# Padding split weight tiles and every second split residual tile by 64 bytes

## The chip, the cores and the metric

The kernel runs on one core of one Trainium2 chip. The time is the device time of one execution in microseconds, from the first to the last instruction with what lies around them. The engines are TensorE (PE, with its weight loads shown apart as PEld), VectorE (DVE), ScalarE (ACT), GpSimd (POOL) and SyncE (SP, which issues DMAs). On-chip memory (SBUF) has 128 partitions; an address below is the byte offset within a partition.

## The reference

512 tokens of 1024 channels in float32 pass through three blocks: a block of two layers with recurrent mixers, a block with two kinds of attention, and a block with latent attention and a convolution branch. Almost all of the arithmetic is products of the normed tokens with weight matrices:

```python
def conv_glu(u, w_in, conv_w, conv_b, w_out):
    gate, val = jnp.split(u @ w_in, 2, axis=-1)
    return (jax.nn.silu(dwconv_centred(gate, conv_w, conv_b)) * val) @ w_out
...
    for i in range(DEPTH):                      # first block
        u = rmsnorm(h, norm1_w[i])
        ... h = h + hgrn2_mixer(u, ...)  or  h + mamba2_mixer(u, ...)
        h = h + conv_glu(rmsnorm(h, norm2_w[i]), ffn_w_in[i], ...)
...
        x = x + jnp.square(jax.nn.relu(h @ w_ff1[i])) @ w_ff2[i]    # second block
...
    a, b = jnp.split(h @ w_13, 2, axis=-1)      # third block, swiglu
    return (jax.nn.silu(a) * b) @ w_2
```

## The kernel before

Channels lie on partitions: the residual is eight tiles `x0` to `x7` of 128 channels by 512 tokens. A float32 product is made from two parts of each operand in the type float32r, high and low: `split` (L241) has ScalarE copy a tile into the high part (L242) and VectorE subtract it from the source into the low part (L243). For the residual these are `xh` and `xl`, eight tiles each, made by `split_tiles` (L272) in the pool `res`; within the feed-forward stages the hidden tiles are `hh` and `hl`, elsewhere `yh`/`yl`, `ogh`/`ogl`, `mh`/`ml`, `mg`, `at`, `oah`/`oal`, `obh`/`obl`, `qah`/`qal`, each in a pool of its stage.

Weights come by `chunk` (L161): one DMA of up to 512 KB into `raw` (128 partitions by 1024 elements, three buffers), then the split into `whi` and `wlo` (three buffers each, used in turn), all in the pool `wp`. `accumulate` (L181) then makes for each k-tile three matmuls into one PSUM bank: `whi` against `xh` (L188), `whi` against `xl` (L189), `wlo` against `xh` (L190). The weights are loaded into the array (128 by 128); the residual tile streams past, 512 columns. Every matmul has a weight load of its own. `tok_unit` (L1098) does it the other way round for a few products: the token tile is loaded and the weights stream, 256 columns (L1110 to L1112), and `products_n` has the same three lines as L1595 to L1597.

All of it is written out as a straight program; the order of PE's instructions is that of the calls, and buffers are waited for where they come round again.

Where tiles lie in SBUF follows from the sizes alone. Pools are laid out in the order in which they are opened, within a pool the tags in the order of their first use, and each tag's buffers side by side, rounded to 32 bytes. `const` comes first, then `res` (`x0` to `x7`, then `xh` 0, `xl` 0, `xh` 1, `xl` 1 and so on, 2048 bytes each), `wp` (`raw`, `whi`, `wlo`, 4096 bytes each), `tp` (temporaries), and then the pool or pools of the running stage. All of `res` and `wp` are multiples of 512 bytes, so `xh`, `xl`, `raw`, `whi` and `wlo` all start at the same place mod 512. The small tiles in `tp` add up to 192 over a multiple of 512, and some stages open small tiles ahead of their large ones. Counted from the place of `whi`, mod 512 bytes:

| tiles | place |
|---|---|
| `x`, `xh`, `xl`, `raw`, `whi`, `wlo` | 0 |
| `yh`, `yl` (mamba, 320 bytes of small tiles ahead) | 0 |
| `hh`, `hl` of `conv_glu` and `relu_ffn`; `mh`, `ml`, `mg`, `at`, `oa`, `ob`, `kvh`, `kvl` | 192 |
| `qah`, `qal` (64 bytes of small tiles ahead) | 256 |
| `hh`, `hl` of `swiglu` (128 bytes of small tiles ahead) | 320 |
| `ogh`, `ogl` (192 bytes of small tiles ahead) | 384 |

Of the kernel before, what the change touches and what calls it, by code (L numbers as in the profile page):

```python
# [9 lines left out]
F32R = mybir.dt.float32r  # L10
# [6 lines left out]
P = 128  # L17
D = 1024
NT = 512
# [3 lines left out]
WSZ = 1024  # L23

# Vectors over channels, kept as columns [128, rows] after a transpose on chip.
# [16 lines left out]
def view(t, off, dims):  # L42
    """The tile's partitions with another pattern of its free elements."""
    return bass.AP(t.tensor, t.offset + off, [t.ap[0], *dims])


def tree_masks():
    """masks[l][s, t]: s and t lie in different halves of one block of 2 ** (l + 1) tokens."""
    import numpy as np

    a = np.arange(P)
    out = np.zeros((8, P, P), np.float32)
    for l in range(7):
        half = a >> l
        out[l] = (half[:, None] ^ half[None, :]) == 1
    return out


def bucket_rows():
    """Rows of buckets against places: place w holds the bias of distance 255 - w; the last row  # L60
    masks the places outside the window."""
    import numpy as np

    out = np.zeros((33, 384), np.float32)
    for w in range(384):
        d = 255 - w
        if not 0 <= d < 128:
            out[32, w] = -1e30
            continue
        b = d if d < 16 else min(31, 16 + int(math.log(d / 16) / math.log(8) * 16))  # L70
        out[b, w] = 1.0
    return out


def rope_consts():
    """The signed swap of channel halves (transposed, for two heads of 64) and cos, sin by channel."""
# [17 lines left out]
class Net:  # L94
# [66 lines left out]
    def chunk(self, w, k0, nk, *segs):  # L161
        """Rows k0.. (nk tiles of 128) of w and the columns in segs (start, count), side by side,
        split into two float32r parts."""
# [5 lines left out]
        hi = self.wp.tile([P, WSZ], F32R, tag="whi", name=self.nm("whi"), bufs=3)  # L169
        lo = self.wp.tile([P, WSZ], F32R, tag="wlo", name=self.nm("wlo"), bufs=3)  # L170
# [10 lines left out]
    def accumulate(self, ps, tile, m, xs):  # L181
        """Add the products of one weight tile's 128 columns m to ps[feature, token]."""
# [9 lines left out]
    def products(self, tiles, m, xs, evac):  # L192
        """evac(psum[feature, token]) of the 128 columns m of weight tiles [(first k, count, parts)]."""
# [5 lines left out]
    def units(self, w, xs, n0, ncols, evac, k0=0):  # L199
        """The calls that make evac(psum, m) for each tile of 128 columns of w: psum[feature, token]  # L200
        over the k-tiles xs; one call for each load of weights."""
# [4 lines left out]
        for c0 in range(n0, n0 + ncols, wide):  # L206
            nn = min(wide, n0 + ncols - c0)

            def unit(c0=c0, nn=nn):
# [4 lines left out]
                # A load is done with before the next one's turn, for all of its columns.  # L214
# [17 lines left out]
    def load(self, w, nk, *segs):  # L232
        """Weight tiles for products: all nk k-tiles of the columns segs."""
# [12 lines left out]
    def begin_norm(self, wname=None, wj=0, via=None, pool=None):  # L246
        """Start of a norm's statistics; prep(j) then takes each tile of x as it is ready, and
        splits its product with the norm's weights where wname is given. via: the weights of a
        norm in between, whose result x becomes (through, once end_norm has its statistics)."""
# [22 lines left out]
    def split_tiles(self, j):  # L272
        h = self.res.tile([P, NT], F32R, tag=f"xh{j}", name=self.nm("xh"))
        l = self.res.tile([P, NT], F32R, tag=f"xl{j}", name=self.nm("xl"))
        return h, l

    def through(self):
        """x becomes the result of the norm in between."""
# [20 lines left out]
    def rsqrt(self, out, v, n):  # L299
        """out = v ** -0.5 on [128, n] columns, with a Newton step."""  # L300
# [9 lines left out]
    def bcast_cols(self, out, cols, nt=4):  # L310
        """[128 tokens, nt] columns to rows [128, nt * 128] that are the same on every partition."""
# [8 lines left out]
    def end_norm(self, want_bc=True, beside=None):  # L320
        """rsqrt(mean(x * x) + eps): columns [128 tokens, 4], and the same broadcast over partitions;
        with a norm in between, both norms' factors together. beside: other work, to go between."""
# [13 lines left out]
        if self.via:  # L336
            # 1 / sqrt(v) / sqrt(s / v + eps) = 1 / sqrt(s + eps * v)
# [14 lines left out]
    def load_x(self, x, *first):  # L352
        """x with channels on partitions. first: weights to load and split on the way."""
# [225 lines left out]
    def gla_steps(self, hp, masks, S, h):  # L579
        """Both directions of one head, in steps that other work may go between.  # L580
        f: [backward, forward] decays; kk: [forward, backward] keys.
        In a chunk of 128 tokens att[s, t] is the sum over channels of q[t] k[s] and the decays between
        the two, found by halves: a pair (s, t) belongs to the one block of 2m tokens in whose halves
        it lies apart."""
# [17 lines left out]
        while m < P:  # L602
            # Keys that the two halves' queries meet, side by side.
# [32 lines left out]
        # Between chunks of 128 tokens by the states that enter them.  # L636
# [35 lines left out]
        # The head's norm, with tokens on partitions; then its gate, and split for the product behind.  # L672
# [22 lines left out]
    def mamba(self, nxt):  # L695
# [6 lines left out]
        with ExitStack() as st:  # L702
# [4 lines left out]
            # silu(t) = h * (1 + tanh(h)) with h = t / 2: the norm's factor and the conv's bias carry the half.  # L707
# [12 lines left out]
            for d, sg in ((0, 1), (1, -1)):  # L720
                # Forward keeps keys s <= t, backward s >= t.
# [25 lines left out]
            def project(g):  # L747
                """The calls that make the group's B, C, x and gate, one for each 128 columns."""
# [44 lines left out]
            def scale(js):  # L793
                """The later groups' operands carry the norm's factor."""
# [22 lines left out]
            while ended < G:  # L817
# [11 lines left out]
                # The last group's chain keeps some for its end.  # L829
# [8 lines left out]
    def mamba_decays(self, mc, mp, dram, w_in, xw, rhalf):  # L838
        """Step sizes and decays of all heads: rows hold [half of the tokens, direction, head]."""
        nc, I = self.nc, self.I  # L840
        H2, NH = 64, NT // 2
        # The heads' columns twice: every half of the rows has all tokens, and keeps its own.
# [24 lines left out]
        # log(1 + e) = 2 atanh(s), s = e / (2 + e) <= 1 / 3, by its series.  # L867
# [16 lines left out]
        # Sums of the log decays in each chunk of 128 tokens, up to t (forward) and from t on (backward).  # L884
# [3 lines left out]
        for hs in halves:  # L888
# [5 lines left out]
            # A chunk's whole sum, for each direction.  # L894
# [18 lines left out]
        # The same with tokens on partitions: [token, chunk, (direction, head)].  # L913
# [8 lines left out]
        # exp of the chunks' sums on every partition.  # L922
# [14 lines left out]
    def ssd_steps(self, mp, g, r, dec, tri, dsk, yo):  # L937
        """Four heads that share B and C: both directions' scans by chunks, the gate and the norm,
        in steps that other work may go between."""
# [15 lines left out]
        def weights(w, hd):  # L955
            """exp(-relu(cum[s] - cum[t])) times the masked products of C and B."""
# [7 lines left out]
        # Tokens on partitions.  # L964
# [12 lines left out]
        # Products of C and B inside each chunk, for the two directions.  # L977
# [11 lines left out]
        def scaled(name, c, dirs, bufs):  # L989
            """x times a factor of each token and head, for the directions dirs."""  # L990
# [10 lines left out]
        # States that enter each chunk.  # L1001
# [96 lines left out]
    def tok_unit(self, w, segs, xs, scale, out):  # L1098
        """out[c][token, column]: the product with tokens on partitions, scaled by token, for the
        256 columns segs."""  # L1100
# [15 lines left out]
    def attention2(self, nxt):  # L1116
# [5 lines left out]
        with ExitStack() as st:  # L1122
# [8 lines left out]
            with ExitStack() as st2:  # L1131
# [22 lines left out]
                def do_wq(i):  # L1154
                    # Window heads i and i + 4 share a tile, so that each lies beside its keys.
# [75 lines left out]
            # The two branches through their gates.  # L1231
# [32 lines left out]
    def window_rows(self):  # L1264
        """For each head the bias by place (bucket_rows), in DRAM, from where a skewed read makes
        [query, 256 keys] of a block of it, the queries from last to first."""
# [15 lines left out]
    def window_steps(self, pool, q, k, vb, e, sinks, ob, h):  # L1282
        """Blocks of 128 queries, from last to first, against their own and the previous block's keys."""
# [46 lines left out]
        # Keys on partitions: own block, then the previous one.  # L1330
# [18 lines left out]
    def stick_steps(self, pool, q, k, va, h, oa):  # L1349
        """a[t, s] = sigmoid(z[t, s]) * prod of sigmoid(-z[t, j]) over s < j < t."""  # L1350
# [48 lines left out]
    def relu_ffn(self, nxt, beside):  # L1399
        """beside: an iterator of other work, to go between the products."""  # L1400
# [36 lines left out]
    def token_embed(self, pp, beside):  # L1437
        """x += (p @ w_pe) * sigmoid(norm(x) @ w_pg); then the statistics of the norms behind.
        beside: an iterator of other work, to go between the products."""
# [19 lines left out]
        def embed(m):  # L1459
            """Products of two tiles, in banks that the others don't wait for."""  # L1460
# [24 lines left out]
    def modulation(self):  # L1485
        """silu(c) @ w_mod + b_mod as columns of channels: six parts for x, two for the context."""
# [35 lines left out]
        # Gain times (1 + scale), to go with the shift.  # L1522
# [7 lines left out]
    def modulated(self, gain, shift0, space=None):  # L1530
        """xw = x * r * gain + shift, split."""
# [13 lines left out]
    def context(self, pool):  # L1545
        """The context's tokens, normalised and modulated: split tiles [channel, 256 tokens] in
        self.cx; in steps."""
# [38 lines left out]
    def products_n(self, tiles, ms, xs, n, pool="mm"):  # L1586
        """As products, for n tokens and the columns ms; returns the sums."""
# [12 lines left out]
    def stat_cols(self, sq, nt, dim):  # L1600
        """rsqrt(mean + eps) as columns [128 tokens, nt] of the squares' sums sq."""
# [574 lines left out]
```

## Time and profile before

| | us |
|---|---|
| time, median of 2 runs | 3435.94 (3434.68 to 3437.2) |
| span of the profiled execution | 3434.3 |
| PE busy in it | 3363.7 (98%) |
| VectorE busy | 2259.7 (66%) |
| ScalarE busy | 1464.2 (43%) |
| GpSimd busy | 69.2 (2%) |

Busy time is the union of an engine's instructions. PE's matmuls overlap one another in the records, so the mean duration of one is longer than the step from one start to the next. "Granted clock" is the share of TensorE's full 2.4 GHz. The profiled execution's span lies 1.6 us under the median of the runs.

### The profile page before, as it was taken

What the parts mean: (1) busy time and instruction counts of PE and PEld (TensorE: products, weight loads), DVE (VectorE), ACT (ScalarE), POOL (GpSimd) and SP (SyncE); (2) the same over time, 40 slices, a digit from 0 to 9 for tenths busy, and PEclk for the clock granted to TensorE, in tenths of its full rate; (3) what the DMA queues carried; (4) which work ended last, traced back from release to release, by engine and by line L of the source; (5) the groups of instructions that cost most, each with busy time, mean ns of one, the idle gap of its engine ahead of it and who ended that gap; (6) DMA issues with size and microseconds to landing.
All of it is one profiled execution on the core that took longest, in us unless ns stands there. A gap on an engine that the chain in (4) does not pass through costs nothing.

```text
span 3434.3 us, 42607 instructions
## 1 busy us (share of the span) xinstructions
PE 3363.7 (98%) x16365; PEld 2754.9 (80%) x16365; DVE 2259.7 (66%) x3509; ACT 1464.2 (43%) x2505; POOL 69.2 (2%) x110
## 2 busy tenths in 40 slices
PE   8999999997999999999999999999999999999998
PEld 6888788885888877888877778888778888888887
DVE  5777756467878877465555587665778889654334
ACT  4344433234655544233455432233546656332223
POOL 0000000000000000000011100000000000000000
PEclk9999999998999999999999999999999999999999
DMA  4222233332534432332332364642422223422332
GB/s 118 79 62 62 69 98 93 98 92 71 139 114 124 116 117 86 98 93 94 94 83 79 100 201 160 195 149 91 119 72 75 79 73 99 141 86 94 97 98 74
DMA packets 409962, 350.43 MB, mean 102 GB/s; under 512 B 33704, under 2 KB 373407, under 8 KB 409759
## 3 DMA queue, kind: packets, MB, share of 16 engines
q1 hardware_dynamic: 405173, 345.42, 33.4%
q8 instruction: 129, 2.11, 0.3%
q10 hardware_dynamic: 4586, 2.29, 0.2%
q14 instruction: 74, 0.61, 0.1%
HBM read 333.75 MB, written 12.86 MB: 101 GB/s over the span
## 4 chain that ended last, share of the span: by engine, by line
PE 81%; DVE 3%; ACT 1%; DMA 1%; issue 1%; POOL 0%; SPq 0%; ACTq 0%; POOLq 0%; DVEq 0%
PE mm L188 22%; PE mm L190 22%; PE mm L189 22%; PE aux L1980 2%; PE aux L1043 2%; PE aux L2013 1%; PE aux L2004 1%; PE aux L1368 1%; PE aux L315 1%; PE aux L1010 1%; PE mm L1595 1%; PE mm L1596 1%; PE aux L1065 1%; PE mm L1597 1%; PE aux L1393 1%
## 5 line engine op out<-in xcount | busy, mean ns | idle before, releaser
L188 PE MATMUL mm<-xh,whi 128*128 128x512 f32 x2584 | 1024.7, 397 | 3.8 <-ACT whi L242 2.4
L189 PE MATMUL mm<-xl,whi 128*128 128x512 f32 x2584 | 1012.9, 392 | 6.7 <-DVE xl L243 4.9
L190 PE MATMUL mm<-xh,wlo 128*128 128x512 f32 x2584 | 1012.0, 392 | 7.2 <-DVE wlo L243 7.2
L242 ACT ACTIVATE whi<-raw 128x1024 fp32r<-128x1024 f32 (+3 forms) x532 | 541.8, 1020 | 1095.6 <-PE mm L189 846.1
L243 DVE TENSOR_TENSOR wlo<-raw,whi 128x1024 fp32r<-128x1024 f32 (+3 forms) x532 | 625.1, 1176 | 511.7 <-ACT whi L242 503.3
L188 PEld LDWEIGHTS mm<-xh,whi 128*128 128x128 f32 x2584 | 487.4, 189 | 116.4 <-issue 11.8
L190 PEld LDWEIGHTS mm<-xh,wlo 128*128 128x128 f32 x2584 | 486.8, 188 | 113.0 <-DVE wlo L243 10.1
L189 PEld LDWEIGHTS mm<-xl,whi 128*128 128x128 f32 x2584 | 487.0, 188 | 106.8 <-DVE xl L243 5.2
L188 PE MATMUL mm<-hh,whi 128*128 128x512 f32 x784 | 309.6, 395 | 0.0
L190 PE MATMUL mm<-hh,wlo 128*128 128x512 f32 x784 | 308.6, 394 | 0.0
L189 PE MATMUL mm<-hl,whi 128*128 128x512 f32 x784 | 308.0, 393 | 0.0
L1916 DVE SCALAR_TENSOR_TENSOR cv<-cu,taps,cv 128x511 f32<-128x511 f32 (+14 forms) x240 | 177.9, 741 | 4.4 <-ACT cv L1912 0.7
L190 PEld LDWEIGHTS mm<-hh,wlo 128*128 128x128 f32 x784 | 146.8, 187 | 35.9
L189 PEld LDWEIGHTS mm<-hl,whi 128*128 128x128 f32 x784 | 146.8, 187 | 35.0
L188 PEld LDWEIGHTS mm<-hh,whi 128*128 128x128 f32 x784 | 146.9, 187 | 34.4
L393 DVE TENSOR_TENSOR x<-x,mm 128x512 f32<-128x512 f32 x136 | 93.1, 686 | 97.5 <-PE mm L190 97.3
L960 ACT ACTIVATE w<-w,mb_cum 128x128 f32<-128x128 f32 x256 | 80.9, 392 | 72.5 <-DMA w<-mb_rows 65.0
L242 ACT ACTIVATE hh<-t 128x512 fp32r<-128x512 f32 x98 | 61.4, 627 | 87.3 <-DVE t L430 57.5
L243 DVE TENSOR_TENSOR hl<-t,hh 128x512 fp32r<-128x512 f32 x98 | 67.6, 690 | 42.0 <-ACT hh L242 41.8
L1509 DVE SCALAR_TENSOR_TENSOR acc<-wm,silu_c,acc 128x512 f32<-128x512 f32 x112 | 81.1, 750 | 6.2 <-DMA wm<-in_w_mod_dram 4.8
L737 DVE SCALAR_TENSOR_TENSOR cy<-mm,cols,cy 128x510 f32<-128x510 f32 (+1 forms) x112 | 83.4, 746 | 1.6 <-ACT cy L733 1.0
L1043 PEld LDWEIGHTS aux<-w,xd 128*64 128x64 f32 x512 | 54.9, 137 | 12.2 <-issue 5.0
(517 smaller groups left out, 4681.6 us busy)
## 6 DMA issues: line engine op xcount, KB each, us to landing
raw<-in_ffn_w_in_dram SPq DMA_DIRECT2D x88, 512.0 KB
raw<-in_w_in_dram SPq DMA_DIRECT2D x69, 512.0 KB
raw<-in_w_ff_dram SPq DMA_DIRECT2D x64, 512.0 KB
raw<-in_w_dram SPq DMA_DIRECT2D x64, 512.0 KB
raw<-in_b_w_in_dram SPq DMA_DIRECT2D x48, 512.0 KB
wm<-in_w_mod_dram SPq DMA_DIRECT2D x48, 512.0 KB
raw<-in_a_w_in_dram SPq DMA_DIRECT2D x40, 512.0 KB
raw<-in_ffn_w_out_dram SPq DMA_DIRECT2D x40, 512.0 KB
```

The source lines that it names most:

```text
L188: nc.tensor.matmul(ps, hi[:, k, ms], xh, start=a + k == 0, stop=False)
L189: nc.tensor.matmul(ps, hi[:, k, ms], xl, start=False, stop=False)
L190: nc.tensor.matmul(ps, lo[:, k, ms], xh, start=False, stop=a + k == len(xs) - 1)
L242: self.nc.scalar.activation(hi, src, AF.Copy)
L243: self.nc.vector.tensor_tensor(out=lo, in0=src, in1=hi.bitcast(F32), op=ALU.subtract)
L393: self.nc.vector.tensor_tensor(out=self.xT[j], in0=self.xT[j], in1=ps, op=ALU.add)
L737: nc.vector.scalar_tensor_tensor(out=y[:, to], in0=src[:, at], scalar=cw(tap, j), in1=y[:, to], op0=ALU.mult, op1=ALU.add)
L960: nc.scalar.activation(w[:, d, c, :], w[:, d, c, :], AF.Relu, scale=-1.0, bias=dec["cum"][:, c, h : h + 1])
L1043: nc.tensor.matmul(py[64 * hh : 64 * hh + 64, cs[c]], xd[c][:, d, hd, :], w[:, d, c, :], start=d == 0, stop=d == 1)
L1509: nc.vector.scalar_tensor_tensor(out=ac, in0=t[:, kk], scalar=col, in1=ac, op0=ALU.mult, op1=ALU.add)
L1916: nc.vector.scalar_tensor_tensor(out=y[:, dst], in0=u[:, src], scalar=taps[:, 15 + o : 16 + o], in1=y[:, dst], op0=ALU.mult, op1=ALU.add)
L1980: nc.tensor.matmul(ps[:, :n], a, b, start=i == 0, stop=i == 4)
```

## The change

`PAD = 16` elements (64 bytes) are added to each buffer of `whi` and `wlo`, and to the buffers of `xl` with an odd index; the tiles' contents and all instructions keep their shapes, as the padding is cut off again by slices. `raw` and `xh` are not padded. Comments and docstrings are blanked line for line; with the line for `PAD`, every line number below it grows by one.

```diff
 WC = 256
 WSZ = 1024
+PAD = 16
@@ chunk
         raw = self.wp.tile([P, WSZ], F32, tag="raw", name=self.nm("raw"), bufs=3)
-        hi = self.wp.tile([P, WSZ], F32R, tag="whi", name=self.nm("whi"), bufs=3)
-        lo = self.wp.tile([P, WSZ], F32R, tag="wlo", name=self.nm("wlo"), bufs=3)
+        hi = self.wp.tile([P, WSZ + PAD], F32R, tag="whi", name=self.nm("whi"), bufs=3)
+        lo = self.wp.tile([P, WSZ + PAD], F32R, tag="wlo", name=self.nm("wlo"), bufs=3)
         cut = lambda t: t[:, :size].rearrange("p (a n) -> p a n", n=nn)
@@ split_tiles
         h = self.res.tile([P, NT], F32R, tag=f"xh{j}", name=self.nm("xh"))
-        l = self.res.tile([P, NT], F32R, tag=f"xl{j}", name=self.nm("xl"))
-        return h, l
+        l = self.res.tile([P, NT + PAD * (j % 2)], F32R, tag=f"xl{j}", name=self.nm("xl"))
+        return h, l[:, :NT]
```

## Rows read from the trace of the kernel before

**Rows 1.** The page, parts 1 and 2: engines' busy time, granted clock by slices.
```profile
PE 3363.7 (98%) x16365; PEld 2754.9 (80%) x16365; DVE 2259.7 (66%) x3509; ACT 1464.2 (43%) x2505; POOL 69.2 (2%) x110
...
PEclk9999999998999999999999999999999999999999
```

**Rows 2.** Who PE waited for: us in total, times, longest.
```profile
PE aux L315 <- DVE rcolx L308: 11.8, 8, 3.8
...
PE mm L190 <- DVE wlo L243: 7.6, 7, 2.2
```

**Rows 3.** Matmul groups by line and tile: busy us, mean ns, idle before.
```profile
L188 PE MATMUL mm<-xh,whi 128*128 128x512 f32 x2584 | 1024.7, 397 | 3.8 <-ACT whi L242 2.4 <-ACT xh L242 0.9 <-ACT xh L265 0.4
...
L188 PE MATMUL mm<-hh,whi 128*128 128x512 f32 x784 | 309.6, 395 | 0.0
...
L1110 PE MATMUL mm<-whi,xh 128*128 128x256 f32 x192 | 54.3, 283 | 0.0
L188 PE MATMUL mm<-yh,whi 128*128 128x512 f32 x128 | 52.4, 414 | 2.1 <-ACT yh L242 2.1
...
L188 PE MATMUL mm<-mh,whi 128*128 128x512 f32 x64 | 25.3, 396 | 0.0
...
L1595 PE MATMUL mm<-xh,whi 128*128 128x512 f32 x48 | 18.5, 392 | 1.3 <-ACT xh L1541 1.3
...
L188 PE MATMUL mm<-qah,whi 128*128 128x512 f32 x36 | 14.6, 407 | 0.0
...
L188 PE MATMUL mm<-oah,whi 128*128 128x512 f32 x32 | 12.7, 396 | 0.0
```

**Rows 4.** Dense `xh` stretches: length, PE, PEld, DVE, ACT, POOL (counts), clock, DMA.
```profile
413.41:492.54 79.13, 79.13 (x351) 65.53 (x349) 52.98 (x69) 29.21 (x37) 0.00 (x0) 1.00 0.31 94
537.56:624.40 86.84, 86.84 (x385) 71.88 (x383) 55.83 (x71) 31.30 (x39) 0.00 (x0) 1.00 0.31 97
```

**Rows 5.** The same for `hh` (first) and `mh`.
```profile
492.76:537.33 44.57, 44.57 (x192) 35.72 (x191) 15.92 (x17) 9.00 (x9) 0.00 (x0) 1.00 0.31 95
...
2003.45:2048.01 44.56, 44.56 (x192) 35.91 (x191) 43.74 (x63) 17.86 (x24) 0.00 (x0) 1.00 0.65 207
```

**Rows 6.** The same for `hh` of `swiglu`.
```profile
3145.16:3188.89 43.73, 43.73 (x192) 35.87 (x191) 16.35 (x17) 9.01 (x9) 0.00 (x0) 1.00 0.30 96
```

**Rows 7.** The same for `og` (first) and `qa` (two stretches).
```profile
387.01:395.84 8.83, 8.83 (x40) 7.16 (x38) 7.75 (x13) 7.23 (x11) 0.10 (x1) 1.00 0.00 0
2723.91:2727.55 3.64, 3.64 (x18) 3.00 (x16) 1.33 (x5) 3.61 (x8) 0.00 (x0) 1.00 0.76 258
2818.86:2822.49 3.63, 3.63 (x17) 3.00 (x16) 1.32 (x5) 3.60 (x8) 0.00 (x0) 1.00 0.36 106
```

**Rows 8.** Timeline in the second stretch of rows 4: start us, us, engine, line.
```profile
539.85 0.39 PE L189 MATMUL mm<-xl,whi 128*128 128x512 f32 x1
539.85 0.19 PEld L190 LDWEIGHTS mm<-xh,wlo 128*128 128x128 f32 x1
```

**Rows 9.** A stretch as in rows 4, of L1010 alone on PE.
```profile
845.06:846.14 1.08, 1.08 (x6) 0.94 (x5) 0.55 (x1) 1.08 (x3) 0.00 (x0) 1.00 1.11 212
```

**Rows 10.** Timeline of PE inside the `mh` stretch of rows 5.
```profile
2004.14 0.40 PE L188 MATMUL mm<-mh,whi 128*128 128x512 f32 x1
2004.38 0.39 PE L189 MATMUL mm<-ml,whi 128*128 128x512 f32 x1
```

**Rows 11.** Stretches as in rows 4 of L1110 to L1112: `xh`, then `kvh` twice.
```profile
1699.59:1721.42 21.83, 21.83 (x183) 21.83 (x183) 5.72 (x12) 9.72 (x20) 0.00 (x0) 1.00 0.27 80
2672.55:2676.55 4.00, 4.00 (x36) 4.00 (x35) 2.35 (x4) 3.60 (x8) 0.00 (x0) 1.00 0.39 86
2852.34:2855.74 3.40, 3.40 (x33) 3.40 (x31) 3.29 (x6) 3.11 (x7) 0.00 (x0) 1.00 0.20 77
```

**Rows 12.** The page, part 5: the split's VectorE groups.
```profile
L243 DVE TENSOR_TENSOR wlo<-raw,whi 128x1024 fp32r<-128x1024 f32 (+3 forms) x532 | 625.1, 1176 | 511.7 <-ACT whi L242 503.3
...
L243 DVE TENSOR_TENSOR hl<-t,hh 128x512 fp32r<-128x512 f32 x98 | 67.6, 690 | 42.0 <-ACT hh L242 41.8
```

## The prediction

> **What bounds the kernel now.** The page comes first: PE is busy 3363.7 of 3434.3 us, at a granted clock of 0.9 and more in every slice but one, VectorE 66%, ScalarE 43% [rows 1]. The list of what PE waits for is short: its largest entry is 11.8 us, and all waits for the weights' low part come to 7.6 [rows 2]. So the time is the number of matmuls times the pace at which PE starts them, and a change moves the end only through that pace or through new waits. By count, the three lines of `accumulate` (L188 to L190) rule: 2584 on each line with the stream `xh` or `xl`, 784 on each with `hh` or `hl`, 128 with `yh`, `yl`, then 64 each for `mh`, `mg`, `at` and `og` (four like the row shown), 32 for `oa` and `ob` (two like it), 36 for `qa` [rows 3].
>
> The "mean ns" of a group (397, 395) is no pace: matmuls overlap. I take the pace from dense stretches, in which PE does nothing but one kind of product: length over the number of weight loads. Two of `xh`: 79.13 us over 349 and 86.84 over 383, both 226.7 ns [rows 4]. One of `hh` and one of `mh`: 44.56 over 191 = 233.3 [rows 5]. `hh` of the last stage (`swiglu`): 43.73 over 191 = 229.0 [rows 6]. `og`: 8.83 over 38 = 232.4; `qa`: 3.63 over 16 = 226.9 and 3.64 over 16 = 227.5, so 227.2 [rows 7]. All at clock 1.00 and with the same 128x512 matmul. Streaming 512 columns at that level (2.4 GHz) is 213.3 ns, so 13 to 20 ns of each are something else.
>
> What differs between these groups is where the streamed tile lies. The timeline shows the weight load of the next matmul starting with the matmul before it (539.85 beside 539.85) [rows 8]: both read SBUF at once. From the tile sizes, weights and `xh`, `xl` start at one place mod 512 bytes (call it 0, with the table ahead of this). Distance, here, is the place of the weights loaded minus the place of the tile streamed, mod 512. Then the trace holds five distances: 0 (`xh`, `yh`) 226.7 ns; 320 (`hh`, `mh`, `mg`, `at`, `oa`, `ob`) 233.3; 192 (`hh` of `swiglu`) 229.0; 128 (`og`) 232.4; 256 (`qa`) 227.2. The stretches of one distance agree though VectorE's load in them runs from 15.92 to 43.74 us of 44.6 [rows 5], which speaks for the place and against the neighbours' traffic. `og` alone is short and lies beside a busy VectorE; its 232.4 is the least sure.
>
> **The change, part by part.** Nothing is added or removed on any engine; only places move.
> (a) Residual tiles. Each odd `xl` slot is 64 bytes longer, so `xh`, `xl` of j = 0, 1 stay at place 0, 2, 3 go to 64, 4, 5 to 128, 6, 7 to 192, and all behind by 256.
> (b) Weights. `raw` (unpadded) goes to 256; the three `whi` to 256, 320, 384; the three `wlo` to 448, 0, 64. Four places and six: the ten of the title. All pools behind move by 640, which is 128 mod 512: `hh`, `mh` and their like from 192 to 320, `hh` of `swiglu` from 320 to 448, `og` from 384 to 0, `qa` from 256 to 384, `yh` from 0 to 128.
> (c) Two of three matmuls are followed by a load of `whi` (L188, L190), one by `wlo` (L189); the three buffers turn evenly. For `xh` this gives, in twelfths, behind `whi`: 64 once, 128 twice, 192 three times, 256 three times, 320 twice, 384 once; behind `wlo`: 0 twice, 64 once, 256 once, 320 twice, 384 three times, 448 three times. Distances 64, 384 and 448 have no row. Bounds: below, the nearest step that PE keeps with another kind of matmul of like length, L1010's 1.08 us for 5 = 216 ns [rows 9]; above, the longest single step inside a dense stretch, 0.24 us = 240 (2004.14 to 2004.38) [rows 10]. I take 230, the middle of the five measured paces' extremes (226.7 and 233.3), as these are the same instruction at the nearest distances.
>
> The sum (change of pace times matmuls):
> - `xh`, `xl`: behind `whi` (3 x 227.2 + 2 x 233.3 + 3 x 229.0 + 2 x 232.4 + 2 x 230) / 12 = 230.0, behind `wlo` (2 x 226.7 + 227.2 + 2 x 233.3 + 7 x 230) / 12 = 229.8; together 229.9, so +3.2 ns. 3 x 2584, and 3 x 48 more of L1595 to L1597, are 7896 matmuls: +25.4 us.
> - `yh`: 3 x 128, new mean 230.1: +1.3 us.
> - `hh` and its like at 233.3 now: 3 x (784 - 176) + 3 x (64 + 64 + 64 + 32 + 32) = 2592 (176 of the 784 are those of `swiglu`). Behind `whi` 448, 0, 64, behind `wlo` 128, 192, 256: mean 229.1, -4.2 ns: -10.9 us.
> - `swiglu`'s `hh`: 528, mean 230.6, +1.6 ns: +0.9. `og`: 192, -2.6 ns: -0.5. `qa`: 108, +2.2 ns: +0.2.
> - L1110 to L1112 stream weights against `xh` by 256 columns. At distance 0 they pace 21.83 / 182 = 119.9 ns; against `kvh` (192) 4.00 / 34 = 117.6 and 3.40 / 30 = 113.3 [rows 11] (one load of each count began earlier). A quarter of the new pairs lie at 0 or 256; with 117 for the rest the mean falls by 2.2 ns, times 576 (three lines like the row of L1110 in [rows 3]): -1.3 us.
> Sum +15 us. With the three open distances at 216 it is -41 - 4 = -45 us, at 240 +57 us.
>
> A rule of the skill speaks against any effect. The rows say 226.7 ns at one place and 233.3 at another with the same instruction at clock 1.00 [rows 4, 5]. The Trainium skill, "TensorE: Matmul & The Clock Gate", section "Step-by-step: what each phase is for", has it that the array has two independent SBUF read ports, so that loading the next weights takes no bandwidth from the running matmul. By it the sum is 0 us; by the rows it is +15. The trace does not agree with it as far as the pace depends on the place. Its section "Back-to-back issue gap" gives N / 2.4 + 2.5, which is an estimate of 215.8 ns here; no dense stretch of these products shows it.
>
> Two edits I cost at nothing. `raw` moves by 256 bytes under the DMA's writes; loads take a share of 0.31 in the dense stretches [rows 4], so even twice that fits, and PE's wait for `wlo` is 7.6 us in all [rows 2]. The split's engines read and write other places: 532 splits of mean 1176 ns on VectorE [rows 12]; half a tile (`hl`, another place) takes 690, which is no sign of a place; 0.1 us more on each would be 53 us inside VectorE's 1174 us of idle time. If that cover failed, L190 would wait on `wlo`.
>
> **The rivals.**
> - The place is not the cause, and the groups' paces differ by something else in their stages. For it: the two-port rule above, which is a mechanism of this kernel too (no stall, no change). Against it: 233.3 holds for `hh` and for `mh`, stages with unlike work beside them. Time 3436. Chance 0.15.
> - The open distances are cheap ones (216 to 225). For it: the 256-column products are quicker off distance 0 [rows 11]. Against: none of the five known is below 226.7. 3391 to 3425. Chance 0.10.
> - Lying at one common place is itself the cost, and all pairs off 0 and 256 run at 220, as the 256-column rows' gain of 6.7 would give (226.7 - 6.7): -76 us, 3360. Against: 320, 128 and 192 have been run at 229 and more. Chance 0.05.
> - The other side, slower. In the kernel before the distance is the same from matmul to matmul through a stage; afterwards it jumps at each change from `whi` to `wlo` and between k-tiles, and PE would have to fall in step anew each time. If every pair off 0 and 256 costs the 233.3 of the worst stretch, +38 us: 3474, chance 0.08. If each costs the single step of 240, +96 us: 3532. It passes 2% from 236.8 ns on (38 us at 233.3 and 8.6 us more per ns). For it: single steps of 0.24 exist [rows 10]; against it: they alternate with 0.23 and no mean is over 233.4. Chance 0.07.
>
> **How the numbers follow.** Forecast, by averaging over distances: chance 0.55, +15 us. The profiled span is 3434.3, 1.6 below the median of 3435.9; the sum is made on the span and carried to the median: 3451 us. Range: from the cheap distances' inner part, 3415, to just past the 233.3 case, 3480; what it leaves out is the 0.05 and 0.07 at the ends and part of the 0.10. The forecast's own range is 3437 to 3465 (the open distances at 226.7 or at 233.3). A change of 2%, 69 us, is about what a measurement of this kernel can tell from none: faster 0.05, within it 0.55 + 0.15 + 0.10 + 0.08 = 0.88, slower 0.07.
>
> **What would show it.** In dense stretches of the profile after: `xh` near 230 in place of 226.7 and no longer the same from chunk to chunk (it repeats over three weight buffers); `hh` near 229 in place of 233.3; the counts, ScalarE's and VectorE's means and PE's waits unchanged. Wrong would be: paces as before (the place is no cause), all near 220 or below (the common place was the cost), `xh` over 236 (the jumps cost), or a new wait of PE for `wlo`.

## The result, and the profile after

The changed kernel takes 3472.35 us (median of 2 runs, 3471.88 to 3472.82), against 3435.94 before: a ratio of 1.0103 [1.0086, 1.012], 36.4 us longer. That is less than the bound of 2%, but the interval lies wholly above 1: the changed kernel is slower by a little more than 1%. The forecast was 3451 us: the sign and the range held, the size did not, +15 us forecast against +36.

The first two fences are from the page of the changed kernel (part 1, PEclk of part 2, three groups of part 5) and from its list of what PE waited for (us in total, times, longest). They answer [rows 1], [rows 3], [rows 12] and [rows 2].

```profile
PE 3402.6 (98%) x16365; PEld 2760.4 (80%) x16365; DVE 2261.9 (65%) x3509; ACT 1466.9 (42%) x2505; POOL 69.2 (2%) x110
...
PEclk9999999998999999999999999999999999999999
...
L189 PE MATMUL mm<-xh,whi 128*128 128x512 f32 x2584 | 1035.3, 401 | 3.1 <-ACT whi L243 1.9
...
L244 DVE TENSOR_TENSOR wlo<-raw,whi 128x1024 fp32r<-128x1024 f32 (+3 forms) x532 | 625.4, 1176 | 522.9 <-ACT whi L243 513.2
...
L189 PE MATMUL mm<-hh,whi 128*128 128x512 f32 x784 | 309.6, 395 | 0.0
```

```profile
PE aux L316 <- DVE rcolx L309: 11.8, 8, 3.8
...
PE mm L191 <- DVE wlo L244: 7.9, 6, 2.7
```

What the reader is to see: PE is busy 38.9 us longer (3402.6 against 3363.7) with the same number of matmuls and the same clock, while its waits (11.8 and 7.9 us), the split's mean of 1176 ns and VectorE's busy time (2 us more) have not moved. So the time went into PE's own pace. The `xh` group is 10.6 us longer, the `hh` group exactly as before: no gain there.

The windows of the changed kernel show the pace (columns as in [rows 4]; in the order `xh`, `hh` of `conv_glu`, `mh`, `mg`, `hh` of `swiglu`, `og`).

```profile
541.28:630.18 88.90, 88.90 (x385) 71.93 (x383) 55.95 (x71) 31.68 (x39) 0.00 (x0) 1.00 0.30 95
741.98:772.40 30.42, 30.42 (x133) 24.63 (x131) 19.20 (x26) 13.46 (x20) 0.00 (x0) 1.00 0.32 93
2028.28:2044.81 16.53, 16.53 (x72) 13.35 (x71) 16.42 (x24) 6.92 (x9) 0.00 (x0) 1.00 0.67 219
3035.21:3079.55 44.34, 44.34 (x193) 35.93 (x191) 25.29 (x32) 17.59 (x23) 0.00 (x0) 1.00 0.29 95
3310.61:3332.68 22.07, 22.07 (x97) 17.86 (x95) 8.45 (x9) 4.76 (x5) 0.00 (x0) 1.00 0.29 96
388.92:397.66 8.74, 8.74 (x40) 7.14 (x38) 7.68 (x13) 7.17 (x11) 0.10 (x1) 1.00 0.00 0
```

Length over steps: `xh` 88.90 / 383 = 232.1 ns (226.7 before, [rows 4]; forecast 229.9), `hh` 30.42 / 131 = 232.2 and `mh` 16.53 / 71 = 232.8 (233.3 before, [rows 5]; forecast 229.1), `mg` 44.34 / 191 = 232.1, `hh` of `swiglu` 22.07 / 95 = 232.3 (229.0 before, [rows 6]; forecast 230.6), `og` 230.0 (232.4 before, [rows 7]). Every product has come to nearly the same 230 to 233 ns. Before, each had the pace of its place.

Where the 36.4 us lie can be summed from the trace. For each matmul of `accumulate` I took the time from its start to the start of PE's next matmul, and added it up by the tile streamed. `xh` and `xl` (7896 steps): 1865.3 us before, 1900.7 after, +35.3. `hh`, `mh` and their like: +0.2 (547.1 to 547.9 for `hh`, -0.2 for `mh` and `mg`, -0.4 for `at`, `oa`, `ob`). `yh` +1.2; the 256-column products of `tok_unit` -0.5; everything else under 1 us. So the change costs 35 us where the distance was 0, and gains nothing where it was 320.

### The profile page after: what moved, and what is told of

It is laid out like the page before. It is cut to its first block, busy times and chain, and to the rows that moved or that the text cites. A ratio compares the mean times of both kernels' runs of the same rounds, so it can differ in the third digit from the quotient of the medians.

```text
span 3471.1 us, 42607 instructions
## 1 busy us (share of the span) xinstructions
PE 3402.6 (98%) x16365; PEld 2760.4 (80%) x16365; DVE 2261.9 (65%) x3509; ACT 1466.9 (42%) x2505; POOL 69.2 (2%) x110
## 4 chain that ended last, share of the span: by engine, by line
PE 83%; DVE 2%; ACT 1%; issue 1%; DMA 1%; POOL 0%; SPq 0%; ACTq 0%; POOLq 0%; DVEq 0%
PE mm L189 23%; PE mm L191 23%; PE mm L190 23%; PE aux L1981 2%; PE aux L1044 2%; PE aux L2014 1%; PE aux L2005 1%; PE aux L316 1%; PE aux L1369 1%; PE aux L1011 1%; PE aux L1066 1%; PE mm L1596 1%; PE mm L1597 1%; PE mm L1598 1%; PE aux L1394 1%
## 5 line engine op out<-in xcount | busy, mean ns | idle before, releaser
L189 PE MATMUL mm<-xh,whi 128*128 128x512 f32 x2584 | 1035.3, 401 | 3.1 <-ACT whi L243 1.9
L190 PE MATMUL mm<-xl,whi 128*128 128x512 f32 x2584 | 1023.7, 396 | 6.8 <-DVE xl L244 4.9
L191 PE MATMUL mm<-xh,wlo 128*128 128x512 f32 x2584 | 1022.5, 396 | 7.5 <-DVE wlo L244 7.5
L244 DVE TENSOR_TENSOR wlo<-raw,whi 128x1024 fp32r<-128x1024 f32 (+3 forms) x532 | 625.4, 1176 | 522.9 <-ACT whi L243 513.2
L189 PEld LDWEIGHTS mm<-xh,whi 128*128 128x128 f32 x2584 | 488.0, 189 | 126.1 <-issue 11.8
L191 PEld LDWEIGHTS mm<-xh,wlo 128*128 128x128 f32 x2584 | 486.3, 188 | 124.8 <-DVE wlo L244 9.7
L191 PE MATMUL mm<-hh,wlo 128*128 128x512 f32 x784 | 310.3, 396 | 0.0
L191 PEld LDWEIGHTS mm<-hh,wlo 128*128 128x128 f32 x784 | 147.3, 188 | 34.7
```

The lines of the kernel that those rows point to most:

```text
L189: nc.tensor.matmul(ps, hi[:, k, ms], xh, start=a + k == 0, stop=False)
L190: nc.tensor.matmul(ps, hi[:, k, ms], xl, start=False, stop=False)
L191: nc.tensor.matmul(ps, lo[:, k, ms], xh, start=False, stop=a + k == len(xs) - 1)
L244: self.nc.vector.tensor_tensor(out=lo, in0=src, in1=hi.bitcast(F32), op=ALU.subtract)
```

## The experiments

All are the kernel before with an edit of places alone; no instruction of PE changes. A gap tile is a small buffer that nothing but one memset touches, put ahead of others so that they lie further on. Line numbers in them are some lines higher. Unless said otherwise a time is one run, set beside runs of the kernel before on the same chip: 3436.09 (first four), 3438.98 (next four), 3436.4 (last three, nine runs from 3432.98 to 3438.29).

Two theories stand behind the expectations. By the first (theory A in the expectations), each pair of weights and stream costs the price of its own distance, whatever came before, and the open distances 64, 384 and 448 are dearer than the 230 ns that I took. By the second (theory B), a change of distance from matmul to matmul costs on top of that. The rival that the place is no cause at all was still to be excluded.

### One distance for all of xh: 64 and 256

```diff
@@ before the first chunk is allocated, in the pool wp
+        self.gap = self.wp.tile([P, 16], F32, tag="gap", name="gap", bufs=1)   # 64 bytes; [P, 64]: 256 bytes
+        tc.nc.gpsimd.memset(self.gap, 0.0)
```

> The kernel before with one unused tile of 64 bytes ahead of raw, whi and wlo: the weights and all behind them move by 64, so the distance of weights to xh is 64 in every matmul and those of the other stages stay. Theory A (each distance has a price, and the open distances 64, 384 and 448 were dearer than assumed): to bring the changed kernel's +36 us they must cost about 235 ns, so xh paces 235 in place of 226.7: 7896 x 8.3 ns = +66 us, 3500 us. Theory B (what costs is that the distance jumps from matmul to matmul; a distance that repeats lets PE settle into a regular step): xh settles between 226.7 and 233.3: 3436 to 3488 us, with one even step through a stretch.

> The same with a tile of 256 bytes: every xh matmul at distance 256. Both theories: 227.2 ns as for qa in the kernel before, +4 us, 3440 us. If the paces belonged to the stages and not to the distance, 3436 us; if 256 is cheap in qa by chance of its neighbours, xh goes to 229 or more, 3454 us or more.

Measured: 3478.39 us with 64 bytes, 3434.84 us with 256. The windows, with 64 bytes (`xh`, then `hh`):

```profile
540.77:630.14 89.37, 89.37 (x385) 72.22 (x384) 56.03 (x71) 31.72 (x39) 0.00 (x0) 1.00 0.30 94
495.97:540.54 44.57, 44.57 (x193) 36.01 (x192) 15.91 (x17) 9.01 (x9) 0.00 (x0) 1.00 0.31 95
```

and with 256 bytes (`xh`, then `hh`):

```profile
535.47:622.30 86.83, 86.83 (x384) 71.94 (x383) 55.84 (x71) 31.30 (x39) 0.00 (x0) 1.00 0.31 97
490.67:535.24 44.57, 44.57 (x193) 35.78 (x192) 15.91 (x17) 9.00 (x9) 0.00 (x0) 1.00 0.31 95
```

Each `xh` window has 383 steps, each `hh` window 191 (where the count of loads is one higher, that load began just before): 233.3 and 226.7 ns for `xh`, 233.4 and 233.4 for `hh`. The weights and the pools behind move together, so `hh` keeps its distance and its pace, although it too lies elsewhere. That settles two things: the place is the cause, as one gap of 64 bytes moves the time by 42 us and one of 256 by nothing; and it is the distance, not the absolute place, since `hh` does not react. Distance 64, one of the three that I had put at 230, costs 233.3.

It also gives the rate of exchange. 6.6 ns in the dense stretches would be 52 us over 7896 steps; the sum of the `xh` steps rose by 44.5. So each ns of dense pace is worth 6.7 us, 0.85 of what counting every matmul gives. Not all steps are as in the window: some 7450 of the 7896 last between 215 and 250 ns, and the mean of these rose by 6.1 ns, from 227.2 to 233.3. With the other gaps of the next section a ns is worth 6.5 to 7.3 us, so what is worked out with 6.7 below is an estimate, good to 2 us or so.

### The other distances: 128, 448, 32, 224

The same edit with gaps of `[P, 32]`, `[P, 112]`, `[P, 8]` and `[P, 56]`.

> As the runs with tiles of 64 and 256 bytes ahead of the weights (xh at 233.3 and 226.7 ns), now 128 bytes. Theory P (the price repeats every 256 bytes): og's 232.4 at distance 128 is the price, +5.7 x 7896 = +45 us, 3481 us. Theory Q (the price rests on where in 512 bytes the distance lies, and og's pace came from its busy neighbours): between 227 and 233, 3438 to 3486 us, with no tie to og.

> 448 bytes, a distance with no row in the kernel before. Theory P: the price of 192, 229.0 ns, +2.3 x 7896 = +18 us, 3454 us. Theory Q: any pace; by the prediction's open value 230 ns, 3462 us; if it is what made the changed kernel dear, 235 ns, 3501 us.

> 32 bytes, half a step. If the price rises evenly from 0 (226.7) to 64 (233.3): 230 ns, +26 us, 3462 us. If 0 is a point of its own: 233, 3486 us. If there is a cheaper place beside 0: under 226 ns, under 3430 us.

> 224 bytes, half a step below 256. If the price falls evenly from 192 (229.0) to 256 (226.7): 227.9 ns, +9 us, 3445 us. If there is a cheaper place just below 0 and 256: under 226 ns, under 3430 us; if 256 is a point of its own: 229 or more, 3454 us or more.

Measured: 3475.82, 3450.81, 3479.63 and 3480.17 us. One `xh` window of each, 383 steps; at distance 128:

```profile
540.27:629.26 88.99, 88.99 (x384) 72.15 (x383) 55.98 (x71) 31.72 (x39) 0.00 (x0) 1.00 0.31 95
```

at 448:

```profile
536.90:624.57 87.67, 87.67 (x385) 71.92 (x383) 55.87 (x71) 31.36 (x39) 0.00 (x0) 1.00 0.31 96
```

at 32:

```profile
541.47:630.83 89.36, 89.36 (x384) 71.94 (x383) 56.02 (x71) 31.77 (x39) 0.00 (x0) 1.00 0.31 94
```

and at 224:

```profile
542.89:632.25 89.36, 89.36 (x384) 71.78 (x383) 56.02 (x71) 31.75 (x39) 0.00 (x0) 1.00 0.31 94
```

Together with the kernel before this is the settled pace, which `xh` keeps when the distance never changes:

| distance | pace, ns | from |
|---|---|---|
| 0, 256 | 226.7 | [rows 4]; `xh` with a gap of 256 |
| 32 | 233.3 | gap of 32 |
| 64, 320 | 233.3 | gap of 64; `hh` in [rows 5] |
| 128 | 232.4 | gap of 128; `og` in [rows 7] |
| 192, 448 | 228.9 to 229.0 | `hh` of `swiglu` in [rows 6]; gap of 448 |
| 224 | 233.3 | gap of 224 |

The pairs 0 and 256, 64 and 320, 192 and 448 agree within 0.1 ns (`qa` at 256, from 16 steps, had 227.2): in these three the pattern repeats with 256 bytes, and for 384 the value of 128 is taken below. 0 is a narrow good place: 32 bytes to either side already cost all there is to lose. Why 192 lies in between is open.

A settled pace is a mean over unlike steps. PE's timeline at distance 128 (start us, us, engine, line) shows one of 0.25 us between others of 0.23:

```profile
560.94 0.40 PE L192 MATMUL mm<-xh,wlo 128*128 128x512 f32 x1
561.17 0.40 PE L190 MATMUL mm<-xh,whi 128*128 128x512 f32 x1
561.42 0.40 PE L191 MATMUL mm<-xl,whi 128*128 128x512 f32 x1
561.65 0.39 PE L192 MATMUL mm<-xh,wlo 128*128 128x512 f32 x1
```

To the nanosecond these steps repeat after seven matmuls (233, 231, 231, 229, 230, 232, 241, give or take 1), and so do those of `og` in [rows 7], at the same distance. At 448 they repeat after three (226, 229, 232). At 64 they alternate between about 231 and 236, and so does `mh` at 320 ([rows 10], where 0.24 us is 236 ns), while `hh` at 320 in [rows 5] has 233 and 234 throughout; the mean is 233.3 in all three. So the distance sets the mean of several matmuls and not each step, and the "one even step" that the second theory expected at 64 is not there.

So the three open distances of the prediction, 64, 384 and 448, are 233.3, 232.4 and 228.9, mean 231.5 where I took 230 (384 by the value of 128). That is dearer, but not by enough: a quarter of the changed kernel's `xh` pairs falls on each of 0, 64, 128 and 192, by this table (226.7 + 233.3 + 232.4 + 228.9) / 4 = 230.3 ns, and the window above shows 232.1.

### Changing distances that are all cheap

```diff
@@ chunk, between the allocation of whi and that of wlo, once
+        if self.n < 8 and not hasattr(self, "gap2"):
+            self.gap2 = self.wp.tile([P, 64], F32, tag="gap2", name="gap2", bufs=1)
+            nc.gpsimd.memset(self.gap2, 0.0)
```

> A tile of 256 bytes between whi and wlo: for xh the loads of whi are at distance 0, those of wlo at 256, so that the distance jumps twice in three matmuls, but only between the two cheap ones. Theory A: xh 2/3 x 226.7 + 1/3 x 227.2 = 226.9 ns; hh has 64 and 320 in turn, about 234.4; 3440 us. Theory B: the jumps cost, xh goes to 231 to 233 ns as in the changed kernel: +34 to +50 us, 3470 to 3486 us.

Measured: 3433.45 us. The `xh` window:

```profile
535.38:622.22 86.84, 86.84 (x385) 71.96 (x384) 55.83 (x71) 31.30 (x39) 0.00 (x0) 1.00 0.31 97
```

86.84 / 383 = 226.7 ns: in every k-tile the distance goes 0, 0, 256, and nothing is lost. So a step between two distances that are the same mod 256 costs nothing, against the 231 to 233 ns of the second theory. By the table ahead, though, such a step is no change at all; what a change mod 256 costs, this run cannot show. A change between unlike places of one price (32, 64 and 224 all have 233.3) was not run.

### Changing distances with different prices

The same edit with `[P, 16]`, 64 bytes in place of 256: `xh` sees the distances 0, 0, 64 in turn, and by their places so do `hh` of `conv_glu` and `mh`.

> A tile of 64 bytes between whi and wlo. For xh the loads of whi are at distance 0 (settled price 226.7), those of wlo at 64 (233.3); hh moves by 64 as well and gets the same pair (256 and 320). Prices alone, one by one: 2/3 x 226.7 + 1/3 x 233.3 = 228.9 ns; xh +2.2 x 7896 = +17 us, hh and its like -4.4 x 2592 = -11 us: 3442 us. Prices that hold only where the distance repeats (theory H: after a jump PE is out of its regular step for several matmuls): about 231 ns in both, +34 - 6 us: 3464 us.

Measured: 3458.85 us. The windows of `xh` (383 steps), `hh` of `conv_glu` (in the second layer) and `hh` of `swiglu` (191 each):

```profile
537.03:625.54 88.51, 88.51 (x385) 72.00 (x383) 55.90 (x71) 31.59 (x39) 0.00 (x0) 1.00 0.30 95
1405.75:1449.89 44.14, 44.14 (x192) 35.90 (x191) 15.93 (x17) 9.00 (x9) 0.00 (x0) 1.00 0.31 95
3162.76:3207.33 44.57, 44.57 (x193) 35.95 (x191) 16.36 (x17) 9.01 (x9) 0.00 (x0) 1.00 0.30 94
```

231.1, 231.1 and 233.3 ns. The settled prices give (226.7 + 226.7 + 233.3) / 3 = 228.9 for the first two, so the mixture costs 2.2 ns per matmul more than its parts. In the third stage the distances are 128, 128, 192, whose prices give 231.2, and it runs at 233.3: 2.1 ns more. The timeline of PE inside the second window (start us, us, engine, line) shows the steps:

```profile
1408.29 0.40 PE L193 MATMUL mm<-hh,wlo 128*128 128x512 f32 x1
1408.53 0.39 PE L191 MATMUL mm<-hh,whi 128*128 128x512 f32 x1
1408.76 0.39 PE L192 MATMUL mm<-hl,whi 128*128 128x512 f32 x1
1408.98 0.40 PE L193 MATMUL mm<-hh,wlo 128*128 128x512 f32 x1
1409.22 0.39 PE L191 MATMUL mm<-hh,whi 128*128 128x512 f32 x1
```

The long step, 0.24 us, is the one from L193 to L191. While L193 streams, the load for L191 runs, that of `whi`, at distance 0: the pair that should be cheapest. The pair at distance 64 (`wlo` loaded while L192 streams) is the step before it. Over about 2400 dense `xh` steps of each kind the means are 229.3 for the step at 64, 235.0 for the first at 0 behind it, 228.7 for the second at 0. So a pair does not have a price of its own: the one at 64 is cheaper than the mean it has alone (233.3), and both at 0 are dearer than theirs (226.7). This goes by the prediction's pairing, of each stream with the load that starts beside it [rows 8]. If each matmul were paired with its own weights, the long step would be that of the pair at 64, and still all three would be dearer than their settled prices; this run does not tell the two pairings apart. By either, over three matmuls the one pair at 64 costs 3 x (231.1 - 226.7) = 13.2 ns, twice the 6.6 that its settled price would add.

### Each half of the change alone

```diff
@@ split_tiles, the residual tiles alone
-        l = self.res.tile([P, NT], F32R, tag=f"xl{j}", name=self.nm("xl"))
-        return h, l
+        l = self.res.tile([P, NT + 16 * (j % 2)], F32R, tag=f"xl{j}", name=self.nm("xl"))
+        return h, l[:, :NT]
@@ chunk, the weights alone
-        hi = self.wp.tile([P, WSZ], F32R, tag="whi", name=self.nm("whi"), bufs=3)
-        lo = self.wp.tile([P, WSZ], F32R, tag="wlo", name=self.nm("wlo"), bufs=3)
+        hi = self.wp.tile([P, WSZ + 16], F32R, tag="whi", name=self.nm("whi"), bufs=3)
+        lo = self.wp.tile([P, WSZ + 16], F32R, tag="wlo", name=self.nm("wlo"), bufs=3)
```

> Only the padding of every second xl: xh and xl of two neighbouring k-tiles share a place, the weights have one place, so the distance is 256, 192, 128, 64 in turn and holds for six matmuls each. Distances of the other stages stay. Theory A with 235 for the open one: (227.2 + 229.0 + 232.4 + 235) / 4 = 230.9 ns, +33 us, 3469 us. Theory B: the distance jumps once in six matmuls, so each part keeps about its settled pace: 228.8 to 230.5 ns, +17 to +30 us, 3453 to 3466 us.

> Only the padding of whi and wlo. For xh the distances are 0, 64, 128 behind whi and 192, 256, 320 behind wlo, for hh 448, 0, 64 and 128, 192, 256. Settled prices one by one (0 226.7, 64 233.3, 128 232.4, 192 228.9, repeating every 256): xh 230.4, +29 us; hh 229.5, -10 us: 3455 us. Theory H: about 232 in both, +41 - 3 us: 3474 us.

Measured: 3469.78 us with the residual tiles alone, 3465.31 with the weights alone. The `xh` window of the first (383 steps):

```profile
539.15:628.04 88.89, 88.89 (x385) 72.02 (x384) 56.01 (x71) 31.61 (x39) 0.00 (x0) 1.00 0.30 95
```

and `xh` (383) and `hh` (191) of the second:

```profile
539.53:627.97 88.44, 88.44 (x384) 71.99 (x383) 55.88 (x71) 31.57 (x39) 0.00 (x0) 1.00 0.30 96
1408.39:1452.87 44.48, 44.48 (x193) 35.95 (x191) 15.91 (x17) 9.01 (x9) 0.00 (x0) 1.00 0.30 95
```

Residual tiles alone: the distance is 0 (256), 192, 128 and 64 for six matmuls each. The table gives 230.3, the window 232.1. Six matmuls are not enough to settle. In dense stretches the six steps at 256 behind those at 64 average 230.1, at 256 behind 192 231.5, against 226.7 settled; those at 192 231, against 228.9; those at 128 and 64 their settled 232.4 and 233.3 within 0.3. What is lost is the cheap distances' advantage. The first theory's 3469 us is met by luck: its mean of 230.9 ns had 235 at distance 64 and 227.2 at 256, where the steps average 233.5 and 230.1 to 231.5.

Weights alone: `xh` has 230.9 where the table gives (2 x 230.8 + 229.6) / 3 = 230.4; `hh` has 232.9 where its pairs (192, 0, 64 behind `whi` and 128, 192, 0 behind `wlo`, mod 256) give 229.5. So in this half alone, too, `hh` does not cash in on its cheaper pairs. Its steps in all went from 547.1 to 548.1 us. The excess over the mean of the prices is thus no fixed sum: 0.5 ns in `xh`, 3.4 in `hh`, and the 3474 us expected from a pace of 232 in both was too much.

The halves cost 33.7 and 28.9 us, and together 36.4, not 62.6: once the cheap place is left for most pairs there is little more to lose.

### All streams at distance 0 or 256

If the distance decides, the tiles that were off it before should gain by being put on it. Gap tiles of 64 bytes ahead of the pools of `conv_glu`, `relu_ffn` and two pools of the second and third block, 128 in `hgrn2`, 192 in `swiglu`:

```diff
@@ conv_glu (relu_ffn and the others alike)
+            gap_ = fp.tile([P, 16], F32, tag="gap", name=self.nm("gap"), bufs=1)
+            nc.gpsimd.memset(gap_, 0.0)
```

> The kernel before, with a small unused tile at the head of each stage's pool (64 bytes in conv_glu, relu_ffn, attention2 and for the third block's gates, 128 in hgrn2, 192 in swiglu), so that hh, mh, mg, at, oa, ob, og too lie at a multiple of 256 from the weights. If the distance is the cause: 233.3 to 226.7 for 2592 matmuls -17 us, 228.9 to 226.7 for 528 -1 us, og 232.4 to 227 for 192 -1 us: 3417 us, 0.994 of the kernel before. If the stages set the pace: no change.

Measured in five rounds: 3418.39 us (median of 5, 3415.1 to 3422.12), ratio to the kernel before 0.9948 [0.9935, 0.9962]: less than 2%, but clear of 1. Windows of `xh` (383 steps), `hh` and `mg` (191 each):

```profile
534.00:620.82 86.82, 86.82 (x384) 71.93 (x383) 55.82 (x71) 31.31 (x39) 0.00 (x0) 1.00 0.31 97
490.49:533.78 43.29, 43.29 (x192) 35.87 (x191) 15.92 (x17) 9.01 (x9) 0.00 (x0) 1.00 0.31 98
2989.71:3033.00 43.29, 43.29 (x192) 35.87 (x191) 25.00 (x32) 17.58 (x23) 0.14 (x1) 1.00 0.30 97
```

All three at 226.7 ns. The steps of `hh` fall by 13.0 us in all, those of `mh` and `mg` by 2.6, of `at`, `oa` and `ob` by 1.7, `xh` stays (+0.1): 17 of the 18 us. This kernel is faster than the kernel before by 18 us, and than the changed kernel, which was not run beside it, by 54 us. It is the change turned round: fewer places, not more.

## Why the forecast went wrong, step by step

**What bounds the kernel: right.** Waits, ScalarE, VectorE and the splits stayed as they were, and all of the change is in PE's pace.

**The place as the cause, by distance: right, and shown.** Gaps of 64 and 256 bytes give 3478 and 3435 us with nothing else changed; the distances in [rows 4] to [rows 7] came back in `xh`, mod 256, with the same prices. With that the first rival (place not the cause) is out, and so are those of cheap open distances and of the common place as the cost: no distance runs under 226.7, and the common place is the best one. As to the two independent read ports of the Trainium skill ("TensorE: Matmul & The Clock Gate", section "Step-by-step: what each phase is for"), by which loading weights takes no read bandwidth from the running matmul: the runs don't agree for this product, as the place of the weights against the stream alone moves the pace from 226.7 to 233.3 ns at a granted clock of 1.00. The 215.8 ns that the prediction works out by the section "Back-to-back issue gap" of that page of the Trainium skill is there the gap of a matmul by itself, not of a stream with a weight load for each.

**The two edits costed at nothing: right.** The mean of the split is 1176 ns on both sides, and the wait for `wlo` 7.9 us.

**The sum over distances: the step that failed.** It took each pair's settled price, and averaged the prices over the pairs as if each matmul paid its own. Three things are in the gap:

- The count. Not all 7896 `xh` steps are dense; the +25.4 us should have been 25.4 x 0.85 = +21.6.
- The open distances, 230 against 231.5 measured. The table's 230.3 for `xh` is 3.6 ns or 24.3 us by the rate of exchange, 2.7 more than 21.6. For `hh` and its like it gives (2 x (228.9 + 226.7 + 233.3) + 232.4 + 228.9 + 226.7) / 9 = 229.5, or -9.8 us, and for `hh` of `swiglu` +1.2: -8.6 together, where I had -10.0.
- The averaging itself. `xh` measured +35.3 against the table's +24.3: 11.0 us more. `hh` and its like measured +0.2 against -8.6: 8.8 us more. Together 19.8 us, by far the largest term.

These come to -3.8 + 2.7 + 1.4 + 19.8 = 20.1 of the 21.4 us by which the forecast was short. The rest is terms near 1 us: the 256-column products gave back 0.5 instead of 1.3, for instance. `yh`'s +1.2, forecast at +1.3, proves nothing, since its steps rose by 0.6 to 1.2 us in every experiment, with all streams at distance 0 or 256 too. The sum's outer values don't quite follow from its terms (with the open distances at 216 and 240 they give -42 and +56 us, not -45 and +57); nothing here rests on that.

That the averaging fails is shown by runs that hold the set of distances small: 0, 0, 64 costs 2.2 ns per matmul above its mean, 0, 0, 256 nothing above it. In the changed kernel even the pairs at distance 0 and 256, singled out among the `xh` steps of 215 to 250 ns, average 232.1 and 232.4 ns.

**The slower rival.** It had PE fall in step anew at each change of distance, 233.3 for all pairs off 0 and 256, and 3474 us. The time is nearly the one measured, and I gave it 0.08. Its mechanism is half right: changes between distances of unlike price do cost beyond their mean, but what is lost sits on the cheap pairs, which it had left at their price, while those at 128 and 192, which it put at 233.3, average 230.9 to 231.5. The two errors nearly cancel, so that its time fits is in part luck. I had set it aside because the single steps of 0.24 us in [rows 10] alternate with 0.23 and no mean was over 233.4. But those rows come from a stretch with one distance all along, and already there the steps are unlike; no row of the kernel before shows what a change of distance does, and for that the open range should have been given more weight than the mean.

**What stays open.** What in the hardware ties one matmul's step to the distance of the pair before. The delay of 235.0 on the step behind the one at 64 and the cycles of two, three and seven steps suggest that load and stream keep a phase to one another which takes several matmuls to be found again; that is argued from the order of the steps, and no run here takes it apart. Whether the excess comes from the unlike prices or from the change of place as such is open too, as no run changes the place mod 256 at one price. Nor is it known why 192 costs a third of what 32, 64 and 224 do.

## What to carry to other kernels

Where the trace shows one matmul shape at two paces and the same clock, compare where the loaded and the streamed operand lie mod 256 bytes before looking at neighbours' traffic. In dense float32r products like these (512 columns streamed, a weight load for each) keep the operands that meet at a multiple of 256 bytes from one another: here a few gap tiles gave 18 us, and padding to spread them cost 36. A cost that is measured in a steady state is not to be averaged over a mixture of states: try the mixture, or give the worst state's price a good part of the chance.

## What the runs showed that was not expected

- One narrow good place: distances of 32 and of 224 mod 256, one step of 32 to either side of 0, cost all of the 6.6 ns.
- The 256-column products, in which tokens are loaded and weights stream, go the other way: distance 0 is the worst of those measured. With the gaps of 32, 64, 128 and 224 the window of L1110 to L1112 runs at 116.7 to 118.6 ns. With the gap of 448, whose distance is 64 for them (token tile minus weights), it has 182 steps (one load of the 183 began before it)

```profile
1706.98:1727.62 20.64, 20.64 (x183) 20.64 (x183) 5.73 (x12) 9.66 (x20) 0.00 (x0) 1.00 0.29 84
```

  of 113.4 ns, against 120.0 in [rows 11], and all of these products together lose 3.4 us, while the `xh` steps rose by 15.1. Other lines' matmuls took 3.4 us more in that trace, so the gain does not show in the whole: the profiled span is 14.8 us above the 3434.3 of the kernel before, and the time 11.8 us above the 3438.98 beside it, two figures that differ by less than the times of the kernel before among themselves. These products are 720 here and those of 512 columns over 11,000, so distance 0 is still the best for the whole.
